# Encoder trunk on one core: low-part matmuls last, second weights loaded earlier, operand splits on VectorE

## The chip, the cores and the metric

One core of a Trainium2 chip runs the whole program in one launch. The metric is the device time of the program in microseconds (us). It is compared between the kernel before and the changed kernel.

## The reference

One layer over 2304 tokens of width 1024 (a sample of 2048 and a prompt of 256), all in float32:

```python
h = rmsnorm(x, norm1_g); p = h @ w_in              # split into q, k, v, g, lr, u, vs, xp
a_out = gla_mixer(...)                             # bidirectional gated linear attention, 512 channels
b_out = spatial_gating(gelu(u), gelu(vs), ...)     # 128x128 position mixing, 256 channels
c_out = pool_mixer(xp, ...)                        # pooling windows 2/4/8/16, 256 channels
x = x + concat([a_out, b_out, c_out]) @ w_o
h = rmsnorm(x, norm2_g)
a, up = split(h @ w_ffn_in, 2)                     # 2816 columns each
a = depthwise_conv3(a, conv_w) + conv_b
x = x + (silu(a) * up) @ w_ffn_out
y = rmsnorm(x, norm_f)
```

## The kernel before, in words

**Numbers in two parts.** A float32 operand of a large product is split into a high part (a copy rounded to TensorE's fp32r format, made by ScalarE) and a low part (the operand minus its high part, made by VectorE or GpSimd): `split`, L162. A product of two split operands is three matmuls into one PSUM bank: high by high, high by low, low by high. `mm3` (L171) issues them in that order for one slice of 128 rows, so they have the lines L172, L173 and L174 in the profile. In the products of the FFN's first matrix the same three stand in L1206 to L1208.

**Stages.** Stage 1 and stage 2 compute the mixers. `out2` (L791) then multiplies by w_o; the last of its runs shares TensorE's time with `hprep` (L964), which makes the first FFN block's token operands. The FFN works on three blocks of tokens. A block has two halves q = 0 and 1 of 384 to 386 columns, and 22 column groups j of the first matrix.

**`ffn1` (L1197)** computes one j by seven products of sums (a Strassen scheme) over four slices kk, 84 matmuls in all. Weight operands are A11, S1 to S4, A12, A22, token operands B11, T1 to T4, B22, B21. `astep` makes one weight operand some products ahead: raw load on SP's queue, high part on ScalarE, low part on GpSimd for S1 to S4 and on VectorE for the rest. In block 0 GpSimd also forms the sums S1 to S4 (L1121). After product 4 VectorE adds bank pD into `u3` (L1215). Product 7 (A22 by T4) writes on in the same bank pD, so its first matmul waits until that add has read it. `gate` (L1220) then runs conv, SiLU and the product on ScalarE and VectorE, and splits the result into uh and ul (L1234, L1236).

**`ffn2` (L1299)** multiplies a part, that is 3 or 4 consecutive j's (`PARTS`), by the second matrix: 8 output groups t, each for q = 0 and q = 1. `loadw2` (L1261) loads a weight group into the two-buffered tile rg, `prepw2` (L1266) splits it into gh (ScalarE) and, two ticks later, gl (VectorE). `before` (L1275) does this for the first two groups while the last `ffn1` ahead of the part runs. There are 21 parts. In the last part of a block the first two groups go in an interleaved order (`late`).

**Block borders.** While the last `ffn1` and last `ffn2` part of a block run, `bload` (L1075) loads the next block's token operands, four pairs p by four slices kk, in the order and at the ticks of `BORDER` (L54), and splits them: high on ScalarE, low on VectorE for p = 0 and 2 and on GpSimd for p = 1 and 3 (L1097). `finish` (L1340) normalises and stores a block's halves; for the very last half `last_norm` (L1377) does so after the last matmul.

**Order of the work.** All queues run in program order. Side work sits in generators on a `Pipe` (L94); `yield d` means "go on d ticks later", and there is one tick for every three matmuls.

Of the kernel before, what the change touches and what calls it, by code (L numbers as in the profile page):

```python
# [26 lines left out]
NJ = DFF // P  # L27
# [20 lines left out]
GD0 = (2, 2, 2, 5, 2, 2)  # L48
GF0 = (0, 1, 1, 2, 1, 1)
GD1 = (2, 2, 2, 2, 2, 2)  # L50
GF1 = (1, 1, 1, 2, 1, 4)
HP = (5, 3, 3, 3)
XG = 30
BORDER = ((0, 2, 13), (1, 2, 16), (2, 2, 19), (3, 2, 22), (0, 0, 42), (0, 1, 45), (1, 0, 48), (1, 1, 52),  # L54
          (2, 0, 56), (2, 1, 60), (3, 0, 64), (3, 1, 68), (0, 3, 78), (1, 3, 82), (2, 3, 86), (3, 3, 90))
BM = (12, 9, 1, 6, 3)
MAN = ("DVE", "Activation", "Pool", "SP")
G1 = (0, 512, 896, 1312)
# [64 lines left out]
def trunk(ctx: ExitStack, tc: tile.TileContext, xT, wa, wb, gw2, gb, rows, wsT, plw, wo, w1, w2, vec, cst, yT):  # L123
# [85 lines left out]
    if True:  # L209
# [8 lines left out]
        xs, post = {}, {}  # L218
# [298 lines left out]
    if True:  # L517
# [273 lines left out]
        def out2(u, get, between=None, begun=None):  # L791
            mh, ml = get()
            n = len(tiles_of[u]) * P
            width = 256
            alloc = lambda name: box2["acc"].tile([P, 256], F32, tag=name, name=name, bufs=AB[name])
            acc = [] if between else [alloc("acc") for _ in range(0, n, width)]

            def sums(c, xf):
                for a, o in zip(acc, range(0, n, width)):
                    w = min(width, n - o)  # L800
                    sq = alloc("sq") if c else a
                    SC.activation(sq[:, 0:w], xf[:, o:o + w], AF.Square)
                    yield 1
                    if c:
                        V.tensor_tensor(out=a[:, 0:w], in0=a[:, 0:w], in1=sq[:, 0:w], op=ALU.add)

            for c in range(KD):
                oh, ol, xr = wx.pop("h"), wx.pop("l"), wx.pop(c)
                pw_ = pmt("pw") if c or not begun else begun
                for k in range(KD):  # L810
                    if c or not begun or k < 4:
                        mm3(pw_[:, 0:n], oh[:, k], ol[:, k], mh[:, k, 0:n], ml[:, k, 0:n], k == 0 and (c > 0 or not begun),
                            k == (3 if begun and not c else KD - 1))
                    if c + 1 < KD and k in (0, 1):
                        wo_split(c + 1, k)
                    if c + 1 + look(u) < KD and k in (3, 5):
                        wo_load(u, c + 1 + look(u), k // 2 - 1)
                    if c + 1 < KD and k == 6:
                        wx[c + 1] = xr_load(u, c + 1)
                    opipe.tick()  # L820
                    (pipe if between else hpipe).tick()
                xf = xr.rearrange("p a t -> p (a t)")[:, 0:n]
                V.tensor_tensor(out=xf, in0=pw_[:, 0:n], in1=xf, op=ALU.add)
                if c + 1 < KD:
                    opipe.add(store(d_x[u][:, c], xf), 1)
# [75 lines left out]
    if True:  # L901
# [173 lines left out]
        def bload(bi, box):  # L1075
            w = box["w"] = width_of(BLOCKS[bi])
            B = box["B"] = btiles()
            got = {}

            def load(kk, p):  # L1080
                m = 2 if p < 3 else 1
                got[kk, p] = xtmp("b")[:, 0:m, 0:w]
                SY.dma_start(out=got[kk, p], in_=d_b[bi, kk][:, 2 * p:2 * p + m, 0:w])

            todo = [(kk, p) for kk, p, _ in BORDER]
            for kk, p in todo[:NX - 1]:
                load(kk, p)
            at = 0
            for n, (kk, p, tick) in enumerate(BORDER):
                if tick > at:  # L1090
                    yield tick - at
                    at = tick
                m = 2 if p < 3 else 1
                hi, src = B[p][:, 0, 0:m, kk, 0:w], got.pop((kk, p))
                SC.activation(hi, src, AF.Copy)
                yield 1
                (GP if p % 2 else V).tensor_tensor(out=B[p][:, 1, 0:m, kk, 0:w], in0=src, in1=hi.bitcast(F32), op=ALU.subtract)  # L1097
                yield 1
# [98 lines left out]
        def ffn1(i, j, box, us):  # L1197
# [2 lines left out]
            fast = j == NJ - 1  # L1200

            def prod(bank, a, b, start):
                for kk in range(4):
                    st = start and kk == 0
                    o, ah, al, bh, bl = bank[:, 0:w], A[a][:, 0, kk], A[a][:, 1, kk], B[BP[b][0]][:, 0, BP[b][1], kk, 0:w], B[BP[b][0]][:, 1, BP[b][1], kk, 0:w]
                    TE.matmul(o, ah, bh, start=st, stop=False, skip_group_check=True)  # L1206
                    TE.matmul(o, ah, bl, start=False, stop=False, skip_group_check=True)  # L1207
                    TE.matmul(o, al, bh, start=False, stop=kk == 3, skip_group_check=True)  # L1208
                    if kk == 0:
                        astep()  # L1210
                    pipe.tick()
                    hpipe.tick()

            def add(out, a, b):
                V.tensor_tensor(out=out, in0=a, in1=b, op=ALU.add)  # L1215
# [56 lines left out]
            yield 2  # L1272
            V.tensor_tensor(out=gl[:, 0:n], in0=rv, in1=gh[:, 0:n].bitcast(F32), op=ALU.subtract)  # L1273

        def before(jobs):  # L1275
            yield 1
            loadw2(jobs[0])
            loadw2(jobs[1])
            yield 12
            begin(prepw2(jobs[0]))  # L1280
            yield 5
            begin(prepw2(jobs[1]))
            yield 2
            loadw2(jobs[2])
            loadw2(jobs[3])

# [12 lines left out]
        def ffn2(jobs, todo, xs, us, no, accs=None, scaled=False, late=False):  # L1299
# [1 line left out]
            n = jobs[0][1]  # L1301
            g = {t: gw.pop(jobs[t]) for t, _ in todo}
            py = {(t, q): (ps if q else pmt)("py") for t, sel in todo for q in sel}
            order = [(t, q, k) for t, sel in todo for q in sel for k in range(n)]
            if late:
                a, b = range(n - 1), range(n)
                order = [(t, q, k) for t, q, ks in ((0, 1, a), (0, 0, a), (0, 1, b[-1:]), (1, 1, b), (0, 0, b[-1:]), (1, 0, b))
                         for k in ks]
            for at, (t, q, k) in enumerate(order):
                x2, c, j0 = xs[q], jobs[t][2], jobs[t][0]  # L1310
                uh, ul = us[j0 + k][q]
                gh, gl = g[t]
                mm3(py[t, q][:, 0:no], gh[:, k], gl[:, k], uh[:, 0:no], ul[:, 0:no], k == 0, k == n - 1)
                if late:
                    if (t, q, k) == (0, 0, n - 1):
                        begin(prepw2(jobs[2]))
                    if at == len(order) - 1:
                        loadw2(jobs[4])
                elif t and at == 0 and t + 1 < len(jobs):
                    begin(prepw2(jobs[t + 1]))  # L1320
                elif t and at == min(4, len(order) - 1) and t + 3 < len(jobs):
                    loadw2(jobs[t + 3])
                pipe.tick()
                bpipe.tick()
                if k < n - 1:
# [51 lines left out]
        def last_norm(blk, q, xs, no, acc):  # L1377
# [14 lines left out]
            SC.activation(col(k), col(k), AF.Copy, scale=vc[:, V_NF + k:V_NF + k + 1])  # L1392
            V.scalar_tensor_tensor(out=r[:, 0:nb], in0=pm[:, 0:nb], scalar=1.0 / D, in1=r[:, 0:nb], op0=ALU.mult, op1=ALU.add)
            GP.tensor_tensor(out=r[:, 0:nb], in0=r[:, 0:nb], in1=mhalf[:, 0:nb], op=ALU.pow)
            for b, c0 in enumerate(starts):
                n = min(P, no - b * P)
                SC.activation(dg[:, b * P:b * P + n], ident[:, P - n:P], AF.Copy, scale=r[:, b:b + 1])
            pipe.flush()
            TE.matmul(pr, ones, dg, start=True, stop=True)
            SC.activation(sq, pr, AF.Copy)  # L1400
            for ks, eng, src, dma in (((0, 1), V, pr, SY), ((2, 3), V, pr, SY), ((6, 7), GP, sq, SC), ((4, 5), V, pr, SY)):
                for k in ks:
# [15 lines left out]
        xs = {}  # L1418
# [7 lines left out]
        for bi, blk in enumerate(BLOCKS):  # L1426
# [5 lines left out]
            for q, n in enumerate(PARTS):  # L1432
# [6 lines left out]
                while todo and todo[0] < min(j0 + n + 1, NJ):  # L1439
# [101 lines left out]
```

## Time and profile before

| | us |
|---|---|
| median of 3 runs (lowest, highest) | 2427.66 (2427.52, 2676.5) |
| profiled execution, its own time | 2424.24 |
| its span, first to last instruction | 2422.5 |
| PE busy in it | 2366.8 |

The profile is of one execution. Its own time lies 1.7 us over its span; the profiled execution is 3.4 us under the median. Engines are PE (TensorE), PEld (its weight loads), DVE (VectorE), ACT (ScalarE), POOL (GpSimd) and SP (the queue that issues most DMAs). "PE fD L1206 <- DVE u L1215" means that a matmul of line 1206 into tile fD stood still until VectorE's instruction of line 1215 had written tile u.

### The profile page before, as it was taken

How to read it: one execution, taken by the hardware profiler on the slowest of the kernel's cores; microseconds unless marked ns; L12 is line 12 of the kernel's file. 1: busy time of each engine (PE TensorE's matmuls, PEld its weight loads, DVE VectorE, ACT ScalarE, POOL GpSimd, SP SyncE). 2: the span in 40 equal slices, each digit the busy share in tenths (PEclk: the TensorE clock that was granted, in tenths of full speed). 3: DMA queues.
4: the chain of work that ended last, by engine and by line, in shares of the span. 5: the costliest groups of instructions: out<-in, count | busy, mean ns of one | idle time of the engine just before them, and what ended most of it. 6: DMA issues, size and time to landing. Idle time of an engine off the chain costs nothing.

```text
span 2422.5 us, 36683 instructions
## 1 busy us (share of the span) xinstructions
PE 2366.8 (98%) x13280; PEld 2258.5 (93%) x13280; DVE 1648.8 (68%) x2899; ACT 1032.7 (43%) x1897; POOL 792.1 (33%) x745
## 2 busy tenths in 40 slices
PE   8999998999999999999999999999999999999997
PEld 7899997988988899999999999999999999999997
DVE  6776667676666786777777686666557765666555
ACT  6454444333333443433344544433336533344434
POOL 3332221111011855455454622323225512222221
PEclk9999999999999999999999999999999999999998
DMA  6343224565663754454535463444335543333323
GB/s 202 132 150 112 82 79 124 181 188 152 209 195 118 231 180 137 151 164 149 155 120 188 131 228 120 144 146 138 111 97 185 180 129 100 96 114 103 111 75 105
DMA packets 225466, 345.99 MB, mean 143 GB/s; under 512 B 25378, under 2 KB 117794, under 8 KB 225284
## 3 DMA queue, kind: packets, MB, share of 16 engines
q1 hardware_dynamic: 218260, 320.69, 42.5%
q0 software_dynamic: 6752, 22.55, 2.5%
q8 instruction: 105, 1.72, 0.3%
q14 instruction: 77, 0.63, 0.1%
q10 hardware_dynamic: 272, 0.39, 0.0%
HBM read 264.30 MB, written 79.25 MB: 142 GB/s over the span
## 4 chain that ended last, share of the span: by engine, by line
PE 81%; DVE 7%; issue 3%; DMA 3%; POOL 3%; ACT 2%; SPq 0%; DVEq 0%; POOLq 0%; ACTq 0%
PE py L174 7%; PE py L173 7%; PE py L172 7%; PE pm L172 4%; PE pm L174 3%; PE pm L173 3%; PE fA L1208 3%; PE fA L1206 3%; PE fA L1207 3%; PE fD L1206 3%; PE fD L1207 3%; PE fD L1208 3%; PE qm L172 2%; PE qm L174 2%; PE qm L173 2%
## 5 line engine op out<-in xcount | busy, mean ns | idle before, releaser
L165 POOL TENSOR_TENSOR S<-S,S 128x512 fp32r<-128x512 f32 x242 | 325.9, 1347 | 709.4 <-ACT S L164 629.5
L174 PE MATMUL py<-uh,gl 128*128 128x384 f32 (+1 forms) x1056 | 358.0, 339 | 6.0 <-DVE gl L1273 6.0
L173 PE MATMUL py<-ul,gh 128*128 128x384 f32 (+1 forms) x1056 | 357.5, 339 | 4.1 <-DVE ul L1236 4.1
L172 PE MATMUL py<-uh,gh 128*128 128x384 f32 (+1 forms) x1056 | 358.3, 339 | 0.6 <-ACT gh L1271 0.6
L1327 DVE TENSOR_TENSOR x<-py,x 128x384 f32<-128x384 f32 (+1 forms) x336 | 186.9, 557 | 180.1 <-PE py L174 178.6
L165 DVE TENSOR_TENSOR A<-A,A 128x512 fp32r<-128x512 f32 x198 | 169.1, 854 | 168.5 <-ACT A L164 147.6
L164 ACT ACTIVATE A<-A 128x512 fp32r<-128x512 f32 x198 | 124.9, 631 | 215.3 <-issue 82.9
L164 ACT ACTIVATE S<-S 128x512 fp32r<-128x512 f32 x242 | 151.9, 628 | 133.3 <-PE fE L1208 67.0
L174 PEld LDWEIGHTS py<-uh,gl 128*128 128x128 f32 x1056 | 199.2, 189 | 8.7 <-DVE gl L1273 8.7
L173 PEld LDWEIGHTS py<-ul,gh 128*128 128x128 f32 x1056 | 199.1, 189 | 5.0 <-DVE ul L1236 4.6
L172 PEld LDWEIGHTS py<-uh,gh 128*128 128x128 f32 x1056 | 199.4, 189 | 1.6 <-ACT gh L1271 0.9
L1271 ACT ACTIVATE gh<-rg 128x384 fp32r<-128x384 f32 (+1 forms) x174 | 93.6, 538 | 231.6 <-PE py L173 207.5
L1206 PE MATMUL fA<-B,A 128*128 128x386 f32 (+1 forms) x528 | 179.4, 340 | 0.0
L1208 PE MATMUL fA<-B,A 128*128 128x386 f32 (+1 forms) x528 | 179.1, 339 | 0.0
L1207 PE MATMUL fA<-B,A 128*128 128x386 f32 (+1 forms) x528 | 178.4, 338 | 0.0
L172 PE MATMUL pm<-wk,xh 128*128 128x512 f32 (+2 forms) x432 | 166.6, 386 | 6.9 <-ACT wk L167 6.6
L173 PE MATMUL pm<-wk,xh 128*128 128x512 f32 (+2 forms) x432 | 157.2, 364 | 0.1
L174 PE MATMUL pm<-wk,xl 128*128 128x512 f32 (+2 forms) x432 | 156.5, 362 | 0.4 <-DVE xl L165 0.4
L1273 DVE TENSOR_TENSOR gl<-rg,gh 128x384 fp32r<-128x384 f32 (+1 forms) x174 | 115.4, 663 | 11.5 <-ACT gh L1271 11.5
L174 PE MATMUL pw<-mh,ol 128*128 128x512 f32 (+1 forms) x320 | 117.9, 368 | 1.5 <-DVE ol L165 1.5
L172 PE MATMUL qm<-vk,xh 128*128 128x512 f32 x288 | 117.9, 409 | 0.0
L172 PE MATMUL pw<-mh,oh 128*128 128x512 f32 (+1 forms) x320 | 117.8, 368 | 0.0
(282 smaller groups left out, 6190.0 us busy)
## 6 DMA issues: line engine op xcount, KB each, us to landing
A<-in_w SPq DMA_DIRECT2D x242, 256.0 KB, 3.8
S<-ds_S SPq DMA_DIRECT2D x176, 256.0 KB, 2.7
rg<-in_w SPq DMA_DIRECT2D x144, 192.0 KB, 2.5
xt<-in_xT SPq DMA_DIRECT2D x35, 512.0 KB, 4.2
ds_S<-S SPq DMA_DIRECT2D x66, 256.0 KB, 2.1
rawo<-dw SPq DMA_DIRECT2D x64, 256.0 KB, 4.4
rg<-in_w SPq DMA_DIRECT2D x30, 256.0 KB, 2.9
dx<-xr SPq DMA_DIRECT2D x24, 256.0 KB, 2.5
```

The source lines that it names most:

```text
L164: SC.activation(hi, src, AF.Copy)
L165: (eng or V).tensor_tensor(out=lo, in0=src, in1=hi.bitcast(F32), op=ALU.subtract)
L172: TE.matmul(out, lh, rhs_h, start=first, stop=False)
L173: TE.matmul(out, lh, rhs_l, start=False, stop=False)
L174: TE.matmul(out, ll, rhs_h, start=False, stop=last)
L1206: TE.matmul(o, ah, bh, start=st, stop=False, skip_group_check=True)
L1207: TE.matmul(o, ah, bl, start=False, stop=False, skip_group_check=True)
L1208: TE.matmul(o, al, bh, start=False, stop=kk == 3, skip_group_check=True)
L1271: SC.activation(gh[:, 0:n], rv, AF.Copy)
L1273: V.tensor_tensor(out=gl[:, 0:n], in0=rv, in1=gh[:, 0:n].bitcast(F32), op=ALU.subtract)
L1327: V.tensor_tensor(out=x2[:, c, 1:1 + no], in0=py[t, q][:, 0:no], in1=x2[:, c, 1:1 + no], op=ALU.add)
```

## The change

Six edits:

1. `out2`: the low-by-high matmul of slice k is issued two slices later.
2. `prod` in `ffn1`: the twelve matmuls of a product go as four high by high, four high by low, four low by high. Ticks and `astep` stay at the same count of matmuls.
3. `ffn2`: for each t all matmuls with gh come first for both halves, then those with gl. The `late` order is rewritten in that sense, with uses of the last j's ul as late as the order allows.
4. `first2` and `before`: the first two loads of rg move from tick 1 of the last `ffn1` ahead of a part to tick 8 of the one before it. Their splits move from ticks 13 and 18 to ticks 3 and 8 (gl two ticks later in each case), the next two loads from tick 20 to tick 12. `GF1` makes the last j's ul three ticks sooner.
5. `bload`: all low parts on VectorE; `BORDER` spreads the 16 splits over ticks 13 to 104 in another order.
6. `last_norm`: `pipe.flush()` comes before the diagonal factors, these are made alternately by ScalarE and VectorE, and each 128-column piece has its own matmul.

```diff
-GF1 = (1, 1, 1, 2, 1, 4)
+GF1 = (1, 1, 1, 2, 1, 1)
-BORDER = ((0, 2, 13), (1, 2, 16), (2, 2, 19), (3, 2, 22), (0, 0, 42), (0, 1, 45), (1, 0, 48), (1, 1, 52),
-          (2, 0, 56), (2, 1, 60), (3, 0, 64), (3, 1, 68), (0, 3, 78), (1, 3, 82), (2, 3, 86), (3, 3, 90))
+BORDER = ((0, 2, 13), (1, 2, 17), (2, 2, 21), (3, 2, 38), (0, 0, 44), (1, 0, 49), (2, 0, 54), (3, 0, 59),
+          (0, 1, 66), (1, 1, 72), (2, 1, 78), (3, 1, 84), (0, 3, 92), (1, 3, 96), (2, 3, 100), (3, 3, 104))
@@ out2
-                    if c or not begun or k < 4:
-                        mm3(pw_[:, 0:n], oh[:, k], ol[:, k], mh[:, k, 0:n], ml[:, k, 0:n], ...)
+                    kn = 4 if begun and not c else KD
+                    if k < kn:
+                        for r in (mh, ml):
+                            TE.matmul(pw_[:, 0:n], oh[:, k], r[:, k, 0:n], start=k == 0 and r is mh and kn == KD, stop=False)
+                        for e in (range(k - 2, k - 1) if k < kn - 1 else range(k - 2, k + 1)):
+                            if e >= 0:
+                                TE.matmul(pw_[:, 0:n], ol[:, e], mh[:, e, 0:n], start=False, stop=e == kn - 1)
@@ bload
-                (GP if p % 2 else V).tensor_tensor(out=B[p][:, 1, 0:m, kk, 0:w], in0=src, in1=hi.bitcast(F32), op=ALU.subtract)
+                V.tensor_tensor(out=B[p][:, 1, 0:m, kk, 0:w], in0=src, in1=hi.bitcast(F32), op=ALU.subtract)
@@ ffn1, prod
+                for n in range(12):
+                    kk, (ia, ib) = n % 4, ((0, 0), (0, 1), (1, 0))[n // 4]
+                    TE.matmul(o, A2[:, ia, kk], B[p][:, ib, e, kk, 0:w], start=start and n == 0, stop=n == 11,
+                              skip_group_check=True)
+                    if n == 2:
+                        astep()
+                    if n % 3 == 2:
+                        pipe.tick()
+                        hpipe.tick()
@@ before
-        def before(jobs):
-            yield 1
+        def first2(jobs):
+            yield 8
             loadw2(jobs[0])
             loadw2(jobs[1])
-            yield 12
+
+        def before(jobs):
+            yield 3
             begin(prepw2(jobs[0]))
             yield 5
             begin(prepw2(jobs[1]))
-            yield 2
+            yield 4
             loadw2(jobs[2])
             loadw2(jobs[3])
@@ ffn2
+            H, M, L = 0, 1, 2
+            if late:
+                a, z = range(n - 1), n - 1
+                runs = [((0, 1), a, (H, M)), ((0, 0), a, (H, M)), ((0, 1), a, (L,)), ((0, 0), a, (L,)), ((1, 1), a, (H, M)),
+                        ((1, 1), a, (L,)), ((0, 1), (z,), (H, L)), ((1, 1), (z,), (H, L)), ((0, 1), (z,), (M,)),
+                        ((1, 1), (z,), (M,)), ((0, 0), (z,), (H, L, M)), ((1, 0), range(n), (H, M)), ((1, 0), range(n), (L,))]
+            else:
+                runs = [((t, q), range(n), f) for t, sel in todo for f in ((H, M), (L,)) for q in sel]
...
+                TE.matmul(py[at][:, 0:no], gv[f == L][:, k], u[f == M][:, 0:no], start=left[at] == 3 * n, stop=left[at] == 1)
...
@@ last_norm
+            pipe.flush()
             for b, c0 in enumerate(starts):
                 n = min(P, no - b * P)
-                SC.activation(dg[:, b * P:b * P + n], ident[:, P - n:P], AF.Copy, scale=r[:, b:b + 1])
-            pipe.flush()
-            TE.matmul(pr, ones, dg, start=True, stop=True)
+                d, e = dg[:, b * P:b * P + n], ident[:, P - n:P]
+                if b % 2:
+                    V.tensor_scalar(out=d, in0=e, scalar1=r[:, b:b + 1], scalar2=None, op0=ALU.mult)
+                else:
+                    SC.activation(d, e, AF.Copy, scale=r[:, b:b + 1])
+                TE.matmul(pr[:, b * P:b * P + n], ones, d, start=True, stop=True, skip_group_check=True)
@@ main loop, ahead of each ffn1
+                    if j == min(j0 + n, NJ - 1) - 1:
+                        pipe.add(first2(jobs))
```

## Rows read from the trace of the kernel before

**Rows 1.** The page: busy us of each engine, share of the span, instructions.

```profile
PE 2366.8 (98%) x13280; PEld 2258.5 (93%) x13280; DVE 1648.8 (68%) x2899; ACT 1032.7 (43%) x1897; POOL 792.1 (33%) x745
```

**Rows 2.** Windows A:B in us: length, busy us of PE, PEld, DVE, ACT, POOL, PEclk, DMA share, GB/s.

```profile
786.00:896.00 110.00, 104.28 (x519) 93.98 (x519) 90.53 (x103) 52.45 (x100) 83.32 (x63) 0.99 0.70 219
2060.00:2160.00 100.00, 100.00 (x567) 100.00 (x566) 63.29 (x107) 43.52 (x80) 26.79 (x20) 1.00 0.36 114
```

**Rows 3.** PE's waits, whole span: total us, times, longest.

```profile
PE fD L1206 <- DVE u L1215: 7.8, 5, 2.0
...
PE py L174 <- DVE gl L1273: 6.0, 8, 2.2
PE py L173 <- DVE ul L1236: 4.1, 2, 2.1
...
PE pr L1399 <- ACT acc L1397: 2.8, 1, 2.8
```

**Rows 4.** PE's waits from 786 to 1300 us (end of out2, most of block 0).

```profile
PE py L174 <- DVE gl L1273: 4.8, 5, 2.2
PE fD L1206 <- DVE u L1215: 4.0, 3, 1.9
PE pw L174 <- DVE ol L165: 1.5, 2, 0.8
PE fE L1208 <- POOL S L165: 0.7, 1, 0.7
PE py L172 <- ACT gh L1271: 0.6, 1, 0.6
```

**Rows 5.** Window just after the stall at 1327 us; columns as in Rows 2.

```profile
1330.50:1333.50 3.00, 3.00 (x12) 3.00 (x11) 0.44 (x1) 0.53 (x1) 0.00 (x0) 0.50 0.00 0
```

**Rows 6.** PE's timeline at 1330 us: start, duration, line, tiles.

```profile
1330.85 0.52 PE L172 MATMUL py<-uh,gh 128*128 128x384 f32 x1
1331.17 0.52 PE L173 MATMUL py<-ul,gh 128*128 128x384 f32 x1
```

**Rows 7.** Timelines of SP, ACT and DVE at 1421 us, block 1.

```profile
1415.01 1.05 SPq L1264 DMA_DIRECT2D rg<-in_w  x2
...
1421.93 0.52 ACT L1271 ACTIVATE gh<-rg 128x384 fp32r<-128x384 f32 x1 [4.86 <-DMA rg<-in_w]
...
1422.48 0.56 DVE L1273 TENSOR_TENSOR gl<-rg,gh 128x384 fp32r<-128x384 f32 x1 [2.82 <-ACT gh L1271]
1422.96 0.55 DVE L1215 TENSOR_TENSOR u<-fD,e 128x386 f32<-128x386 f32 x1
```

**Rows 8.** DVE's timeline at 1035 us, block 0.

```profile
1030.96 1.31 DVE L165 TENSOR_TENSOR A<-A,A 128x512 fp32r<-128x512 f32 x1 [0.86 <-issue]
...
1035.87 1.65 DVE L1273 TENSOR_TENSOR gl<-rg,gh 128x384 fp32r<-128x384 f32 x1
1037.43 0.55 DVE L1215 TENSOR_TENSOR u<-fD,e 128x386 f32<-128x386 f32 x1
...
1039.59 0.54 DVE L1273 TENSOR_TENSOR gl<-rg,gh 128x384 fp32r<-128x384 f32 x1
```

**Rows 9.** Groups of PE by line and shape: count, busy us, mean ns.

```profile
L1208 PE MATMUL fA<-B,A 128*128 128x386 f32 x352 | 119.4, 339 | 0.0
...
L1207 PE MATMUL fA<-B,A 128*128 128x386 f32 x352 | 118.7, 337 | 0.0
```

**Rows 10.** Line 1097, border splits: duration ns min/median/max, first and last start.

```profile
L1097 DVE TENSOR_TENSOR B<-b,B x16: 954/1100/2634, 1317.5 to 1870.3; 128x772 fp32r<-128x772 f32 x8, 128x776 fp32r<-128x776 f32 x8
...
L1097 POOL TENSOR_TENSOR B<-b,B x16: 1013/1450/2642, 1338.0 to 1885.5; 128x772 fp32r<-128x772 f32 x4, 128x386 fp32r<-128x386 f32 x4, 128x776 fp32r<-128x776 f32 x4, 128x388 fp32r<-128x388 f32 x4
```

**Rows 11.** Timeline of the tail, ACT and PE.

```profile
2409.77 1.17 ACT L1397 ACTIVATE acc<-ident,rt 128x128 f32<-128x128 f32 x4 [2.08 <-POOL rt L1394]
...
2411.00 1.66 PE L1399 MATMUL pr<-acc,ones 128*128 128x386 f32 x2 [2.85 <-ACT acc L1397]
```

**Rows 12.** Chain of waits at the end of out2: start, us, what.

```profile
811.65 2.82 POOL B L165 x3
```

More of the change, by code (lines that the diff above doesn't have):

```diff
@@ L810, in out2 @@
                 for k in range(KD):
-                    if c or not begun or k < 4:
-                        mm3(pw_[:, 0:n], oh[:, k], ol[:, k], mh[:, k, 0:n], ml[:, k, 0:n], k == 0 and (c > 0 or not begun),
-                            k == (3 if begun and not c else KD - 1))
+                    kn = 4 if begun and not c else KD
[5 more added lines that the diff above has]
+                                TE.matmul(pw_[:, 0:n], ol[:, e], mh[:, e, 0:n], start=False, stop=e == kn - 1)
                     if c + 1 < KD and k in (0, 1):
@@ L1202, in prod @@
             def prod(bank, a, b, start):
[L1203 to L1209, printed above, removed]
+                o, A2, (p, e) = bank[:, 0:w], A[a], BP[b]
+                for n in range(12):
[3 more added lines that the diff above has]
+                    if n == 2:
                         astep()
-                    pipe.tick()
-                    hpipe.tick()
+                    if n % 3 == 2:
+                        pipe.tick()
+                        hpipe.tick()
             def add(out, a, b):
@@ L1303, in ffn2 @@
             py = {(t, q): (ps if q else pmt)("py") for t, sel in todo for q in sel}
-            order = [(t, q, k) for t, sel in todo for q in sel for k in range(n)]
+            H, M, L = 0, 1, 2
             if late:
[L1306 to L1313, printed above, removed]
+                a, z = range(n - 1), n - 1
[4 more added lines that the diff above has]
+                runs = [((t, q), range(n), f) for t, sel in todo for f in ((H, M), (L,)) for q in sel]
@@ L1314, in ffn2 @@
+            order = [(at, k, f) for at, ks, fs in runs for k in ks for f in fs]
+            left = {at: 3 * n for at in py}
+            for no_, (at, k, f) in enumerate(order):
+                (t, q), x2 = at, xs[at[1]]
+                c, j0 = jobs[t][2], jobs[t][0]
+                u, gv = us[j0 + k][q], g[t]
+                TE.matmul(py[at][:, 0:no], gv[f == L][:, k], u[f == M][:, 0:no], start=left[at] == 3 * n, stop=left[at] == 1)
+                left[at] -= 1
                 if late:
-                    if (t, q, k) == (0, 0, n - 1):
+                    if at == (0, 0) and not left[at]:
@@ L1316, in ffn2 @@
                         begin(prepw2(jobs[2]))
-                    if at == len(order) - 1:
+                    if no_ == len(order) - 1:
                         loadw2(jobs[4])
-                elif t and at == 0 and t + 1 < len(jobs):
+                elif t and no_ == 2 and t + 1 < len(jobs):
                     begin(prepw2(jobs[t + 1]))
-                elif t and at == min(4, len(order) - 1) and t + 3 < len(jobs):
+                elif t and no_ == min(14, len(order) - 1) and t + 3 < len(jobs):
@@ L1322, in ffn2 @@
                     loadw2(jobs[t + 3])
-                pipe.tick()
-                bpipe.tick()
-                if k < n - 1:
+                if no_ % 3 == 2:
+                    pipe.tick()
+                    bpipe.tick()
+                if left[at]:
                     continue
-                V.tensor_tensor(out=x2[:, c, 1:1 + no], in0=py[t, q][:, 0:no], in1=x2[:, c, 1:1 + no], op=ALU.add)
+                V.tensor_tensor(out=x2[:, c, 1:1 + no], in0=py[at][:, 0:no], in1=x2[:, c, 1:1 + no], op=ALU.add)
```

## The prediction

> **What bounds the kernel now.** I read the page first, then the windows by stretch, then PE's waits, then the timelines around the longest waits. The page shows PE busy 2366.8 of 2422.5 us [rows 1]; the next engine, VectorE, has 68%. So PE's own stream sets the time, and an edit of order can win only what PE stands still, 55.7 us in all. The steady stretch of a later block shows PE busy 100.00 of 100.00 us with 567 matmuls, 0.176 us each [rows 2]: there is nothing to win inside a block. What is left sits at places. From 786 to 896 us, the end of `out2` and the first `ffn1`s of block 0, PE is busy 104.3 of 110 us while VectorE has 90.5 and GpSimd 83.3 [rows 2]. The list of waits names the rest: product 7 for `u3` 7.8 us, `ffn2` for gl 6.0 and for ul 4.1, the last broadcast for its diagonal factors 2.8 [rows 3]. Of these, 4.8 of gl and 4.0 of `u3` lie before 1300 us, with 1.5 for `out2`'s low parts, 0.7 for an S operand's low part and 0.6 for gh [rows 4]. A stall can cost twice: after the one at 1327 us the granted clock is 0.50, the lower level of 1.2 GHz, for at least 3 us [rows 5], and matmuls then start 0.32 us apart [rows 6].
>
> All terms go against the profiled execution's own 2424.24 us, which stands 3.4 us under the median of 2427.66; the forecast is the median less the same sum.
>
> **The parts, one by one.**
>
> *gl later (edit 3).* In a group of three j's the first matmul with gl was the 3rd and becomes the 13th; with four j's it becomes the 17th. Ten matmuls at 0.176 are 1.8 us of new slack. The eight waits are at most 2.2 us long [rows 3], so only the longest leaves some 0.4: **-5.6 us**; ends -6.0 and, if VectorE simply stays late, -1.2 (those outside block 0, 6.0 less 4.8 [rows 3, 4]).
>
> *gh.* The buffer of gh is now free six matmuls (1.1 us) before the group ends, so the 0.6 us wait [rows 4] goes: **-0.6**; ends -0.6 and 0.
>
> *ul (edits 3 and 4).* In the `late` order the last j's ul was first used by the 20th matmul and now by the 32nd: 12 x 0.176 = 2.1 us. `GF1` issues it three ticks, nine matmuls, 1.6 us sooner. Together 3.7 us against waits of at most 2.1: **-4.1**. The half clock at 1330 us goes too: 3.0 us at 0.32 are 9.4 matmuls, each 0.144 too slow: **-1.4**. Ends: -5.5 and 0. What is next is the last j's uh, used by the 19th matmul before and by the 28th now.
>
> *Loads of rg sooner (edit 4).* At 1421 us the chain is plain: rg issued at 1415.0, ScalarE waits 4.86 us for it, VectorE stands behind with gl for 2.82, and `u3`, queued behind gl, comes late to product 7 [rows 7]. An `ffn1` has 28 ticks, so tick 8 of the one before is 21 ticks or 11 us sooner than tick 1: the 4.86 are covered, and the two waits outside block 0, 7.8 less 4.0, go [rows 3, 4]: **-3.8**; ends -3.8 and 0. Each part moves four DMA issues on SP's queue, in all 84: the first two past the operand loads of 21 ticks, the others past those of 8. A pair takes 1.05 us to issue [rows 7]; the operand loads behind them are made several products ahead, which hides that; with that cover gone it would be 1.05 us in such a part. The third and fourth load wait for the first two gl, now two ticks after the second gl is issued instead of none, so SP stands less.
>
> *The same move in block 0.* There VectorE is behind without help from a DMA: the gl ahead of `u3` takes 1.65 us and the second gl, after `u3`, 0.54 [rows 8]. The change puts both ahead of `u3`, but earlier, where VectorE has 0.86 us of idle time [rows 8]. `u3` then moves by between -0.9 (the idle time is used and the second gl adds nothing) and +1.65 (it adds a slow one). I take **0** for the 4.0 us of waits, nearest the sum 0.54 - 0.86; ends -5.4 (with a half clock of 1.4 after the longest) and the price of the slower rival below. Here a page bears on it. The Trainium skill, "SBUF — State Buffer", section "Who interferes with whom", says that a VectorE instruction with two SBUF inputs and a GpSimd one that reads SBUF block each other. The trace agrees: the same gl took 1.65 and 0.54 us [rows 8].
>
> *Low parts last in `out2` and `ffn1` (edits 1 and 2).* The waits they reach are 1.5 and 0.7 us [rows 4]. But in that stretch the chain of waits runs over GpSimd's splits [rows 12], and PE relieved at one place comes sooner to `u3`, which VectorE gives no sooner. I take **0**; ends -2.2 and 0. The order itself: of the three matmuls the second shares its weights with the first, and in the new order of a product no neighbours do. Lines 1207 and 1208 differ by 2 ns, 337 and 339 [rows 9], and every matmul has its own weight load, 13280 and 13280 [rows 1]. So 0, with ends of plus and minus 1848 x 2 ns = 3.7 us. The Trainium skill, "TensorE: Matmul & The Clock Gate", section "Part 2: What happens when you issue a matmul", says that weights loaded once can serve many matmuls, which speaks for the old order. By that rule the sum would be 3.7 us worse; by the rows it is not.
>
> *Border splits (edit 5).* GpSimd loses 16 instructions of 1.45 us median, VectorE gains 16 at 1.10 median, 2.63 at most [rows 10]; the eight narrow ones should be less. That is some 9 us of VectorE per border, over 40 ticks (21 us) and more. Outside block 0 VectorE is 63% busy [rows 2], which hides it: **0**. The last four, for T4, now fall in the next block's first `ffn1` at ticks 0 to 12, ahead of product 7 at tick 24, six us later. If the cover is gone, each border waits for one split: +2.6 twice, +5.3. End below: 0, no wait for B stands in the list.
>
> *Tail (edit 6).* The factors take 1.17 us for four, the broadcast 1.66 [rows 11]. The first piece can start after one factor, 0.9 us sooner, and four pieces cost some of it back: **-0.6**; ends -0.9 and +0.8 (half a broadcast for the extra starts).
>
> **Sum:** -5.6 - 0.6 - 4.1 - 1.4 - 3.8 - 0.6 = -16.1 us. The profiled execution would take 2408.1; the median **2411.6 us**.
>
> **Rivals.**
>
> *Block 0 gives its gain back.* VectorE's backlog there comes from GpSimd, not from the order, so the waits for gl and gh return one group later. For it: the slow gl in rows 8. Against: `ffn2` gives VectorE time to catch up. 5.0 us less gain: 2416.6. Chance 0.20.
>
> *Block 0 is cured as well.* The idle 0.86 us is used, `u3` comes in time, and `out2` and S waits pay: another 5.4 + 2.2 = 7.6 us: 2404.0. For it: 0.86 over 0.54. Against: GpSimd's chain [rows 12]. Chance 0.15.
>
> *Slower: the second gl ahead of `u3`.* Place: product 7 of the last `ffn1` ahead of each of block 0's six parts with three j's. Price: 1.65 us for a slow gl [rows 8] plus 1.4 of half clock, 3.05 x 6 = 18.3, and the gains of block 0 are gone: -16.1 + 5.0 + 18.3 = +7.2, 2434.9. It decides once `u3` falls behind by more than the slack that the four parts without a wait have, which no row gives. For it: both splits really go ahead of `u3`. Against: they also go earlier. Chance 0.08.
>
> *The products run slower in the new order.* +3.7: 2415.3. Chance 0.07, since the 2 ns are of the size by which equal groups differ.
>
> *The order does nothing* is not a case of its own: the waits named in rows 3 and 7 follow from it.
>
> **Numbers.** The forecast has 0.50. The range goes from the cured case, rounded down, 2403, to the first rival with the border's 5.3 and some 1 us for the tail, 2423. A difference of 2%, about 49 us, is what a measurement of this kernel can tell from no change. The waits that the edits can reach sum to 7.8 + 6.0 + 4.1 + 2.8 + 1.5 + 0.7 = 22.9 us [rows 3, 4], gh's 0.6 and two half clocks on top, so over 2% faster has 0.02; over 2% slower needs several new waits per part, 0.03; within 2% 0.95.
>
> **What would show it.** Gone from PE's waits: ul, gl outside block 0, and `u3` outside block 0; the clock stays at 1.00 at the end of block 0's last part. gl in block 0 falls under 1 us. If `u3` grows before 1300 us, the slower rival is at work; if waits for gl there stay near 4.8, the first one. The mean of the product matmuls tells the order's price: 341 ns instead of 339 would bear it out. A wait of a product for a B tile's low part after a border would show that VectorE can't hide the splits. The prediction is wrong at its root if PE's busy time per matmul moves, since all terms are waits.

## The result, and the profile after

The changed kernel takes **2408.97 us** (median of 4 runs, 2404.49 to 2411.89) beside 2427.59 for the kernel before on the same chip: a ratio of **0.993 [0.9915, 0.9945]**, 18.6 us less by the medians. One of the four executions of the kernel before took 2676.5 us, a tenth more than the others, and the ratio leaves it out. The difference counts as no change at a bound of 2%, and is faster by the interval. The forecast was 2411.6.

The profiled execution took 2410.87 us. Its page, as in [rows 1]:

```profile
span 2409.1 us, 36723 instructions
PE 2366.8 (98%) x13286; PEld 2263.4 (94%) x13286; DVE 1667.0 (69%) x2917; ACT 1030.9 (43%) x1895; POOL 772.1 (32%) x729
```

The span fell from 2422.5 us. PE does the same matmuls but for six in the tail; what changed is where it stands. That its busy time is the same to the tenth, 2366.8 us, is chance: among the kernels below it lies between 2357.9 (e13_block0_dve) and 2368.2 us (e4_tail). The list of PE's waits over the whole span (total us, times, longest), beside [rows 3]:

```profile
PE fD L1210 <- DVE u L1219: 5.2, 3, 2.2
...
PE pr L1416 <- ACT acc L1415: 2.1, 1, 2.1
...
PE pw L817 <- DVE ol L165: 0.8, 1, 0.8
...
PE py L1324 <- ACT gh L1275: 0.8, 1, 0.8
...
PE py L1324 <- ACT uh L1238: 0.6, 1, 0.6
...
PE py L1324 <- DVE gl L1277: 0.4, 1, 0.4
```

ul is gone, gl fell from 6.0 to 0.4, and `u3` stands at 5.2 us, all three waits in block 0; after 1300 us only uh and the final norm are waited for. Windows of the changed kernel (length, busy us of PE, PEld, DVE, ACT, POOL, PEclk, DMA share, GB/s):

```profile
786.00:896.00 110.00, 105.44 (x526) 95.16 (x524) 90.69 (x112) 52.14 (x101) 80.99 (x62) 0.98 0.69 218
1330.50:1333.50 3.00, 3.00 (x18) 3.00 (x18) 3.00 (x5) 2.30 (x6) 0.98 (x1) 1.00 0.02 5
2060.00:2160.00 100.00, 100.00 (x567) 100.00 (x566) 64.37 (x110) 40.75 (x75) 22.57 (x17) 1.00 0.32 100
72.50:75.50 3.00, 3.00 (x15) 3.00 (x16) 1.31 (x3) 0.77 (x2) 1.34 (x3) 0.50 0.57 214
864.50:867.50 3.00, 3.00 (x11) 3.00 (x10) 2.19 (x4) 1.23 (x2) 2.33 (x2) 0.50 0.78 197
898.50:901.50 3.00, 3.00 (x11) 3.00 (x10) 2.19 (x3) 1.23 (x2) 1.21 (x1) 0.50 0.25 94
840.00:1300.00 460.00, 453.42 (x2550) 450.74 (x2549) 344.90 (x485) 182.73 (x343) 248.43 (x176) 0.99 0.48 152
```

The first three answer to [rows 2] and [rows 5]: the later block is as full as before, and at 1330 us the granted clock is 1.00 where it was 0.50. New are half clocks, that is stretches with a granted clock of 0.50, at 72, 393 and 417 us, in code that the change doesn't touch, and at 864 and 898 us, behind two of the waits for `u3`. In block 0 the kernel before had the one at 894 us and, at the block's end, the one of [rows 5]. The last window in the kernel before:

```profile
840.00:1300.00 460.00, 449.84 (x2529) 445.30 (x2528) 340.88 (x481) 183.01 (x340) 239.22 (x173) 1.00 0.48 149
```

So profiles are best compared by the length of a block, from its first product to the next block's, as PE's timeline shows it (us). The kernel before, run beside each group on its chip, took 2427.18 (e1 to e4), 2429.72 (e5 to e8), 2427.39 (e9, e11) and 2427.26 us (e12, e13).

| Kernel | Median time | Block 0 starts | Block 0 | Block 1 |
|---|---|---|---|---|
| before | 2427.6 | 830.66 | 531.00 | 521.98 |
| after | 2408.97 | 833.80 | 524.23 | 515.41 |
| e1_order | 2418.54 | 832.94 | 524.98 | 517.71 |
| e2_loads | 2415.84 | 834.55 | 524.76 | 517.65 |
| e3_border | 2425.48 | 829.92 | 532.32 | 520.53 |
| e4_tail | 2426.98 | 832.09 | 528.68 | 523.11 |
| e5_old_product | 2407.97 | 830.44 | 523.00 | 515.48 |
| e6_gl1_after_u3 | 2407.89 | 833.28 | 525.10 | 515.42 |
| e7_old_split_ticks | 2413.77 | 834.65 | 526.91 | 515.20 |
| e8_no_sums | 2397.27 (one run) | 833.00 | 511.70 | 515.19 |
| e9_sums_dve | 2401.94 | 830.84 | 516.40 | 515.57 |
| e11_u3_first | 2414.79 | 833.30 | 527.56 | 515.19 |
| e12_before_sums | 2418.28 | 831.16 | 524.96 | 521.80 |
| e13_block0_dve | **2397.14** | 831.34 | 513.17 | 515.19 |

After against before: block 0 starts 3.1 us later (the stages ahead of `out2` end 4.0 later with their three half clocks), block 0 takes 6.8 less, block 1 6.6, block 2 2.6, the tail 0.6: -13.4 in the span. The medians differ by 5.2 more, because before's profile lay 3.4 below its median and after's 1.9 above.

The splits in block 1, ScalarE's and VectorE's timelines beside [rows 7]:

```profile
1410.92 0.51 ACT L1275 ACTIVATE gh<-rg 128x384 fp32r<-128x384 f32 x1
...
1411.46 0.56 DVE L1277 TENSOR_TENSOR gl<-rg,gh 128x384 fp32r<-128x384 f32 x1
1414.64 0.55 DVE L1277 TENSOR_TENSOR gl<-rg,gh 128x384 fp32r<-128x384 f32 x1
1416.77 0.55 DVE L1219 TENSOR_TENSOR u<-fD,e 128x386 f32<-128x386 f32 x1
```

ScalarE waits for no DMA, both gl are done ahead of `u3`, and PE doesn't wait for `u3`. The same place in block 0, VectorE beside [rows 8]:

```profile
888.24 1.57 DVE L1277 TENSOR_TENSOR gl<-rg,gh 128x384 fp32r<-128x384 f32 x1
890.67 1.32 DVE L165 TENSOR_TENSOR A<-A,A 128x512 fp32r<-128x512 f32 x1 [0.39 <-issue]
...
893.47 1.66 DVE L1277 TENSOR_TENSOR gl<-rg,gh 128x384 fp32r<-128x384 f32 x1
896.73 0.55 DVE L1219 TENSOR_TENSOR u<-fD,e 128x386 f32<-128x386 f32 x1
```

Both gl are slow and both stand ahead of `u3`, and PE waits 2.17 us for it: the place of the slower rival. But of PE's three waits for `u3` in block 0 only this one and the one at 1181 us (0.96 us) lie in the last `ffn1` ahead of a part. The other, 2.10 us at 863 us, lies in the block's second `ffn1`, before any gl is made. There a split of an A operand stands ahead of `u3`:

```profile
861.32 1.61 DVE L165 TENSOR_TENSOR A<-A,A 128x512 fp32r<-128x512 f32 x1
862.86 0.55 DVE L1219 TENSOR_TENSOR u<-fD,e 128x386 f32<-128x386 f32 x1
```

### The profile page after: what moved, and what is told of

Its sections match the earlier page's. It is cut to its first block, busy times and chain, and to the rows that moved or that the text cites. A ratio compares the mean times of both kernels' runs of the same rounds, so it can differ in the third digit from the quotient of the medians.

```text
span 2409.1 us, 36723 instructions
## 1 busy us (share of the span) xinstructions
PE 2366.8 (98%) x13286; PEld 2263.4 (94%) x13286; DVE 1667.0 (69%) x2917; ACT 1030.9 (43%) x1895; POOL 772.1 (32%) x729
## 4 chain that ended last, share of the span: by engine, by line
PE 84%; DVE 5%; DMA 3%; POOL 3%; issue 2%; ACT 2%; SPq 0%; DVEq 0%; POOLq 0%; ACTq 0%
PE py L1324 21%; PE fA L1210 10%; PE fD L1210 10%; PE fC L1210 5%; PE fB L1210 5%; PE fE L1210 5%; PE pw L814 4%; PE pm L172 3%; PE pm L173 3%; PE pm L174 3%; PE qm L172 2%; PE qm L174 2%; PE qm L173 2%; PE pw L817 2%; DMA A<-in_w 1%
## 5 line engine op out<-in xcount | busy, mean ns | idle before, releaser
L1210 PE MATMUL fA<-B,A 128*128 128x386 f32 (+1 forms) x1584 | 302.7, 340 | 0.0
L1210 PEld LDWEIGHTS fA<-B,A 128*128 128x128 f32 x1584 | 281.4, 189 | 0.6
L1340 DVE TENSOR_TENSOR x<-py,x 128x384 f32<-128x384 f32 (+1 forms) x336 | 180.1, 557 | 144.9 <-PE py L1324 143.6
L1324 PE MATMUL py<-uh,gl 128*128 128x384 f32 (+1 forms) x1056 | 216.1, 338 | 0.4 <-DVE gl L1277 0.4
L1324 PEld LDWEIGHTS py<-uh,gl 128*128 128x128 f32 x1056 | 187.8, 188 | 1.0 <-DVE gl L1277 0.7
L1210 PE MATMUL fD<-B,A 128*128 128x386 f32 (+1 forms) x792 | 153.0, 342 | 5.3 <-DVE u L1219 5.2
L1210 PE MATMUL fC<-B,S 128*128 128x386 f32 (+1 forms) x792 | 151.2, 339 | 0.0
L1210 PE MATMUL fD<-B,S 128*128 128x386 f32 (+1 forms) x792 | 150.7, 338 | 0.0
L1210 PE MATMUL fB<-B,S 128*128 128x386 f32 (+1 forms) x792 | 150.7, 339 | 0.0
L1210 PE MATMUL fE<-B,S 128*128 128x386 f32 (+1 forms) x792 | 150.7, 339 | 0.0
```

The source lines that it names most:

```text
L1210: TE.matmul(o, A2[:, ia, kk], B[p][:, ib, e, kk, 0:w], start=start and n == 0, stop=n == 11, skip_group_check=True)
L1324: TE.matmul(py[at][:, 0:no], gv[f == L][:, k], u[f == M][:, 0:no], start=left[at] == 3 * n, stop=left[at] == 1)
L1340: V.tensor_tensor(out=x2[:, c, 1:1 + no], in0=py[at][:, 0:no], in1=x2[:, c, 1:1 + no], op=ALU.add)
```

## The experiments

**The parts by themselves.** Each of the first four is the kernel before with one part of the change.

*e1_order*: the orders of `out2`, product and `ffn2` alone.

```
- mm3(...)                          # out2, prod, ffn2
+ runs = [((t, q), range(n), f) for t, sel in todo for f in ((H, M), (L,)) for q in sel]
...
```

> The kernel before with the three new matmul orders alone (out2, product, ffn2). Theory of waits by place: gl in ffn2 has 1.8 us more room, so its 6.0 us fall to about 0.4, gh's 0.6 go, the last j's ul gets 2.1 us of room against waits of 2.1 us, so at most 0.3 of its 4.1 us stay and the half clock at 1330 us goes (1.4); u3's 7.8 us stay, since VectorE's queue is unchanged. Sum 5.6 + 0.6 + 4.1 + 1.4 = 11.7 us: about 2416. Rival, VectorE simply late in block 0: its gl waits (4.8 us) move one group on, gain 6.9: about 2421. Rival, the gain is in loads and border: within 2 us of 2427.6.

2418.54 us, ratio 0.9967 [0.9953, 0.9981]. PE's waits from 786 to 1300 us, against [rows 4]:

```profile
PE fD L1210 <- DVE u L1219: 8.8, 5, 2.4
PE fE L1210 <- ACT S L164: 1.0, 1, 1.0
...
PE py L1322 <- DVE gl L1277: 0.5, 1, 0.5
```

gl falls from 4.8 to 0.5 and `u3` grows from 4.0 to 8.8: in block 0 the order alone moves the wait to another tile. The time lies between the theory's 2416 and the first rival's 2421; the wait came back at `u3`, which the theory left unchanged, and not at gl. The gain is ul, the gl waits of the later blocks, and both half clocks of block 0 (one comes at 1938 us instead).

*e2_loads*: the loads and splits of the second weights sooner, alone.

```
-GF1 = (1, 1, 1, 2, 1, 4)
+GF1 = (1, 1, 1, 2, 1, 1)
+        def first2(jobs):
+            yield 8                # in the ffn1 before
...
```

> The kernel before with the loads and splits of the second weights sooner and the last j's ul three ticks sooner, old matmul orders. Theory of waits by place: the two u3 waits of blocks 1 and 2 go (3.8 us), ul loses 1.6 of each 2.1 us wait (3.2) and with it the half clock (1.4); gl of later groups stays in the main, as their splits are started where they were: gain 8.4 us, about 2419. Rival, the loads alone set the whole gain, gl included: 15 us or more, 2412. Rival, both gl splits ahead of u3 cost as much in block 0 as is won elsewhere: 2425 to 2430, and u3's wait before 1300 us above 6 us.

2415.84 us, 0.9953 [0.9936, 0.997]. PE's waits from 1300 to 2406 us:

```profile
PE py L174 <- DVE gl L1273: 1.4, 3, 0.6
PE py L173 <- DVE ul L1236: 0.9, 1, 0.9
```

No `u3` is left there, and block 1 is 4.3 us shorter. It gained 3 us more than expected: in block 0 `u3` fell from 4.0 to 0.9, and the half clock at 894 us did not come. So with the old order the earlier splits help `u3` there, too.

*e3_border*: the border's ticks and all its splits on VectorE.

```
-(GP if p % 2 else V).tensor_tensor(out=B[p][:, 1, 0:m, kk, 0:w], ...)
+V.tensor_tensor(out=B[p][:, 1, 0:m, kk, 0:w], ...)
```

> The kernel before with the border splits all on VectorE and spread, nothing else. Theory of waits by place: no PE wait hangs on them but ul's, since VectorE has two B splits fewer between ticks 13 and 25 ahead of the last gate; ul's wait falls by about one split, 0.95 us each, and perhaps the half clock: gain 0 to 3.4 us, 2424 to 2428. Rival, the port: GpSimd's 16 splits hold VectorE up, and their removal is worth more than 4 us.

2425.48 us, 0.9993 [0.9982, 1.0003]: no difference. No wait for a B tile appears.

*e4_tail*: the last factors piecewise.

```
-TE.matmul(pr, ones, dg, start=True, stop=True)
+TE.matmul(pr[:, b * P:b * P + n], ones, d, start=True, stop=True, ...)   # in the loop over pieces
```

> The kernel before with the last factors and the last broadcast made piecewise, nothing else. Theory: the wait of 2.8 us before the broadcast falls by 0.7 to 0.9, the broadcast of 1.66 grows by some 0.2: gain 0.6 us, 2427.0. Rival: more matmul starts eat it all, 0.

2426.98 us beside 2427.18, 0.9999 [0.9984, 1.0014]: the 0.6 us can't be seen in times. They stand in after's tail (ScalarE, VectorE and PE), against [rows 11]:

```profile
2396.94 0.69 ACT L1415 ACTIVATE acc<-ident,rt 128x128 f32<-128x128 f32 x2 [2.08 <-POOL rt L1407]
2397.02 0.42 DVE L1413 TENSOR_SCALAR acc<-ident,rt 128x128 f32<-128x128 f32 x2
2397.39 1.86 PE L1416 MATMUL pr<-acc,ones 128*128 128x128 f32 x8 [2.08 <-ACT acc L1415]
```

The factors take 0.69 instead of 1.17 us, the wait falls by 0.77, and the eight pieces cost 0.20 more than the two matmuls.

**What sets `u3` in block 0.** The next four are the changed kernel with one edit each.

*e5_old_product*: the product's old order (hi·hi, hi·lo, lo·hi for each kk).

```
-for n in range(12):
-    kk, (ia, ib) = n % 4, ((0, 0), (0, 1), (1, 0))[n // 4]
+for kk in range(4):
...
```

> The changed kernel with the old order inside a product (high, low, low-by-high for each slice). Theory: inside a product the order is worth nothing but the waits for an S operand's low part (1.5 us with the old order, 0 with the new); u3 in block 0 stands by VectorE's queue, so PE that no longer waits there waits at u3: 2409 within 2 us. Rival: the new product order brings PE sooner to u3 and so costs the two half clocks of block 0: u3 before 1300 us falls from 5.2 to about 1, 2404 to 2406. Rival: the order pays in every product by its cadence: 2413 or more.

2407.97 us, 0.9914 [0.9899, 0.9929]: its interval overlaps that of the change. The order of the product is worth nothing that can be measured in times. In block 0 `u3` is waited for five times, 4.0 us in all and 1.2 at most, S costs 1.2 again, and no half clock comes; the block is 1.2 us shorter than with the change. The Trainium skill, "TensorE: Matmul & The Clock Gate", section "Part 2: What happens when you issue a matmul", says that weights loaded once can serve many matmuls. In both orders every matmul here has its own weight load (13286 of 13286), and these runs show no price of either order.

*e6_gl1_after_u3*: the second split at tick 16, behind `u3`. The next two loads follow it in the same generator, so they move too, from tick 12 to tick 20.

```
-            yield 5
+            yield 13
             begin(prepw2(jobs[1]))
```

> The changed kernel with the second group's split begun at tick 16 instead of 8 of the last ffn1 ahead of a part, so that its gl stands behind u3 on VectorE. Theory: in block 0 that gl (0.55 to 1.65 us) delays u3: u3 before 1300 us falls from 5.2 to about 2 and one half clock goes, 2404 to 2406; gl and ul stay cured, as gl of the second group is used 31 matmuls into the part. Rival: VectorE is behind for another reason, u3 stays near 5: 2409. Rival: gl of the second group is now late: waits for gl above 1.5 us, 2411.

2407.89 us, 0.991 [0.9893, 0.9926]. Inconclusive: `u3` fell to 3.6 and one half clock went, but there are four waits for gh that no theory named, 4.4 us (786 to 1300 us):

```profile
PE py L1324 <- ACT gh L1275: 4.4, 4, 2.0
PE fD L1210 <- DVE u L1219: 3.6, 3, 1.8
```

The first of them, at 904 us, shows time given back. ScalarE started that gh at 903.70 us, behind a step of `gate` that had waited for VectorE; in the changed kernel it started it at 904.88. But PE, held up less at `u3`, came for it at 903.3 instead of 907.4 us.

*e7_old_split_ticks*: loads as in the change, splits at the old ticks.

```
-            yield 3
+            yield 13
             begin(prepw2(jobs[0]))
...
```

> The changed kernel with the first two loads sooner, but their splits at the old ticks 13 and 18 and the next two loads at tick 20. Theory: blocks 1 and 2 were cured by the load being there, not by the split's tick: u3 after 1300 us stays 0; in block 0 it is as with the changed kernel or worse, 5 to 8: 2409 to 2412. Rival: the splits' ticks cured blocks 1 and 2: u3 after 1300 us is back at 3.8, 2413.

2413.77 us, 0.9934 [0.9919, 0.9949]. PE's waits from 786 to 1300 us:

```profile
PE fD L1210 <- DVE u L1219: 7.8, 5, 2.3
PE fD L1210 <- ACT S L164: 0.9, 1, 0.9
```

After 1300 us one wait of 1.0 is left for `u3`, and block 1 is as short as with the change. So in the later blocks it is mostly the early load that cures. In block 0 PE waits 7.8 us for `u3` instead of 5.2, as the theory had it (5 to 8), and the block is 2.7 us longer. By its ratio the run can't be told from the change (0.9934 and 0.993), so that the early splits help in block 0 is read from the profile alone.

*e8_no_sums*: GpSimd's 88 sums for S operands in block 0 are left out (a copy on ScalarE stands for those that don't add in place), so the output differs.

```
-            GP.tensor_tensor(out=out, in0=a, in1=b, op=o)
+            if out is not a and out is not b:
+                SC.activation(out, a, AF.Copy)
```

> The changed kernel with GpSimd's sums S1 to S4 in block 0 left out (S1 and S2 are plain ScalarE copies, S3 and S4 are unchanged tiles, so the output differs). Theory: GpSimd's two-input work holds VectorE up in block 0; without 88 sums of 1.3 to 1.7 us VectorE's 1.6 us instructions there fall to 0.55 to 0.7, u3 before 1300 us falls under 0.5 and gl and gh with it, no half clock in block 0: about 2400. Rival: VectorE's own work is too much there: u3 stays above 3, 2407 or more.

2397.27 us in one run. Window 840 to 1300 us, columns as above:

```profile
840.00:1300.00 460.00, 460.00 (x2615) 459.46 (x2614) 298.56 (x499) 211.92 (x396) 124.38 (x96) 1.00 0.51 159
```

The group of VectorE's splits of A operands in that window (count, busy us, mean ns, idle before):

```profile
L165 DVE TENSOR_TENSOR A<-A,A 128x512 fp32r<-128x512 f32 x62 | 44.2, 714 | 53.7 <-ACT A L164 53.7
```

In the changed kernel the second row was:

```profile
L165 DVE TENSOR_TENSOR A<-A,A 128x512 fp32r<-128x512 f32 x61 | 69.4, 1137 | 43.4 <-ACT A L164 36.0 <-issue 7.4
```

PE is full, no wait for `u3`, gl, gh or S is left in block 0, and VectorE's own split runs in 714 instead of 1137 ns. This points at GpSimd's sums as what made VectorE late; with work left out and one run it takes the next runs to show it.

**Can that be had without leaving work out?**

*e9_sums_dve*: the sums on VectorE (the changed kernel).

```
-            GP.tensor_tensor(out=out, in0=a, in1=b, op=o)
+            V.tensor_tensor(out=out, in0=a, in1=b, op=o)
```

> The changed kernel with block 0's sums S1 to S4 made by VectorE instead of GpSimd. Leaving the sums out took 46 us off VectorE's busy time from 840 to 1300 us; making the 80 there itself at 0.69 each costs it 55. Theory, GpSimd costs VectorE the time its two-input instructions run beside VectorE's: the two about cancel, and VectorE's queue now also waits for the raw loads of the sums: u3 before 1300 us 5 or more, 2409 to 2415. Rival, it is the length of single blocked instructions, not the sum, that makes u3 late: u3 before 1300 us under 2, 2401 to 2404.

2401.94 us, 0.9902 [0.9876, 0.9927], which still touches the interval of the change. My theory, that slower and faster VectorE work would cancel, fell; the rival's time held (2401 to 2404), with `u3` at 2.3 us, a little above the 2 that it named. Window 840 to 1300 us, and VectorE's splits of A operands in it:

```profile
840.00:1300.00 460.00, 456.41 (x2588) 454.47 (x2588) 339.14 (x574) 189.87 (x349) 125.22 (x96) 1.00 0.49 154
L165 DVE TENSOR_TENSOR A<-A,A 128x512 fp32r<-128x512 f32 x61 | 44.2, 725 | 35.7 <-ACT A L164 35.7
```

VectorE does 89 instructions more than in the changed kernel, the sums among them, and is busy 339.1 us instead of 344.9. Another rival, that the sums come sooner and so ScalarE's high parts do too, doesn't explain the splits: VectorE stands idle for ScalarE before them as long as before (35.7 and 36.0 us), and what changed is their length.

*e11_u3_first*: the changed kernel, the operand step of product 7 behind the addition of `u3`.

```
-            prod(pD, "S3", "T3", True)
+            prod(pD, "S3", "T3", True, False)
             u3 = tmp("u3")[:, 0:w]
             add(u3, pD, e1)
+            astep()
```

> The changed kernel with the weight operand that is made during product 4 begun after u3's add instead of before it, in all blocks, so that its low part (0.7 to 1.8 us on VectorE) stands behind u3. Its use is product 7, eight ticks later, and its low part is used only by the last four matmuls there. Theory, u3 in block 0 is late by what stands just ahead of it on VectorE: u3 before 1300 us falls from 5.2 to under 1 and both half clocks of block 0 go: gain 4 to 7 us, 2402 to 2405. Rival, VectorE is behind as a whole and the time is given back at the next user: waits for ul, gl or A operands' low parts of 4 us or more before 1300 us, 2409.

2414.79 us, 0.9948 [0.9928, 0.9969]: the theory fell, though both half clocks of block 0 went as it said. PE's waits from 786 to 1300 us:

```profile
PE fD L1210 <- DVE u L1219: 4.5, 3, 2.4
PE py L1325 <- ACT gh L1276: 3.1, 3, 1.7
PE fE L1210 <- ACT S L164: 1.2, 3, 0.6
```

Little comes off `u3`, and more appears at gh and S, which neither theory nor rival named: this new order of VectorE's queue did not help.

*e12_before_sums*: the kernel before with e9's edit alone.

```
-            GP.tensor_tensor(out=out, in0=a, in1=b, op=o)
+            V.tensor_tensor(out=out, in0=a, in1=b, op=o)
```

> The kernel before with block 0's sums S1 to S4 on VectorE, none of the six edits. Theory, from the run with the sums moved in the changed kernel: single VectorE instructions blocked behind GpSimd's are what makes PE wait in block 0, whatever the order; of the 10.1 us there (gl 4.8, u3 4.0, S 0.7, gh 0.6) with a half clock of 1.4 some 6 to 9 go, u3 under 1 and gl under 3: 2419 to 2421. Rival, the edits have to be there first: u3 and gl before 1300 us stay above 7 together, 2425 or more.

2418.28 us, 0.9966 [0.9952, 0.9979]. Block 0 is 6.0 us shorter and block 1 as before: one line is worth about half of the change. Before 1300 us `u3` falls from 4.0 to 0.2 and gl from 4.8 to 1.8, while the low parts of S, still GpSimd's, grow from 0.7 to 2.6. PE's waits from 1300 us on are those of before:

```profile
PE py L173 <- DVE ul L1236: 4.1, 2, 2.1
PE fD L1206 <- DVE u L1215: 3.9, 2, 2.1
```

*e13_block0_dve*: the changed kernel with e9's edit, and block 0's S splits on VectorE too.

```
-            split(t[:, 0], t[:, 1], src, eng=GP if n[0] == "S" else V)
+            split(t[:, 0], t[:, 1], src, eng=GP if n[0] == "S" and i >= NJ else V)
```

> The changed kernel with block 0's sums and the low parts of its S operands all on VectorE, so that GpSimd does next to nothing in block 0. Theory: the rest of the waits before 1300 us (u3 2.3, gh 1.1, S 0.3 with the sums alone moved) is GpSimd's too and goes: 2398 to 2400. Rival: VectorE, busy 339 of 460 us with the sums, gets some 55 us more less what the contention gave back, and is late by its own work: u3 or gl of 4 us or more before 1300 us, 2404 to 2410.

**2397.14 us** (2395.15 to 2399.69), 0.9882 [0.986, 0.9905]: better than both kernels, its interval clear of the change's. Of the waits for `u3`, gl, gh and S from 786 to 1300 us one is left:

```profile
PE fD L1210 <- DVE u L1219: 1.1, 1, 1.1
```

Window 840 to 1300 us:

```profile
840.00:1300.00 460.00, 458.85 (x2606) 457.89 (x2605) 371.23 (x663) 194.63 (x353) 13.71 (x12) 1.00 0.51 158
```

VectorE's splits of A operands there:

```profile
L165 DVE TENSOR_TENSOR A<-A,A 128x512 fp32r<-128x512 f32 x62 | 42.6, 687 | 10.7 <-ACT A L164 10.4
```

VectorE is busier (371 of 460 us) and, but for one wait, in time; GpSimd is nearly idle.

## Why the prediction was right, and where it was not

The frame held: PE's work is constant and only its standing changed. The parts:

- **gl: -5.6 forecast, 6.0 to 0.4 measured.** Right in size. The reason holds outside block 0. In block 0 e1_order shows that the order alone hands the wait to `u3`; the loads and splits sooner take most of that off again (e2_loads).
- **gh: -0.6 forecast, 0.6 to 0.8 measured.** Wrong in its mechanism: in both kernels ScalarE didn't wait for the buffer there. gh stood in its queue behind ten small instructions of 2.59 us, with no idle time before it. ScalarE's timeline, two rows of the kernel before and two of the changed one:

```profile
969.85 2.59 ACT L1040 ACTIVATE rb<-ident,r 128x1 f32<-128x1 f32 x10
...
973.16 0.51 ACT L1271 ACTIVATE gh<-rg 128x384 fp32r<-128x384 f32 x1
...
974.01 2.59 ACT L1044 ACTIVATE rb<-ident,r 128x1 f32<-128x1 f32 x10
...
977.34 0.51 ACT L1275 ACTIVATE gh<-rg 128x384 fp32r<-128x384 f32 x1
```

- **ul: -4.1 and -1.4 forecast.** The wait went and the clock stays at 1.00, but uh, named as next, took 0.6: -3.5.
- **Loads: -3.8 outside block 0.** Right: gone in e2_loads, down to 1.0 in e7_old_split_ticks with loads alone.
- **`u3` in block 0: 0 forecast, 4.0 to 5.2 measured**, with two half clocks behind these waits where there was one. The prediction weighed the splits alone, between idle time that is used and a slow gl that is added. By themselves they win (4.0 to 0.9 in e2_loads), though in the changed kernel slow gl stand ahead of `u3` at 893 us. What the term left out is the order: PE, no longer held up before, comes sooner to `u3` (8.8 in e1_order). What I had as a backlog has a cause that e8_no_sums and e9_sums_dve show: with GpSimd's sums the same split takes VectorE 1137 ns, without them 714, with the sums on VectorE 725. The Trainium skill, "SBUF — State Buffer", section "Who interferes with whom", says that a VectorE instruction with two SBUF inputs and a GpSimd one that reads SBUF block each other; the runs agree, by those numbers. The prediction used it for one gl and not for the whole block, where 12 us more lay (2408.97 to e13's 2397.14).
- **`out2`, S and the product's order: 0 forecast.** ol fell from 1.5 to 0.8 and S's 0.7 went, 1.4 of the 2.2 that the lower end held. Product matmuls take the same mean time, as the group of the changed kernel shows against [rows 9]:

```profile
L1210 PE MATMUL fA<-B,A 128*128 128x386 f32 x1056 | 201.6, 339 | 0.0
```

- **Border: 0.** Right by e3_border: 16 more splits on VectorE with no wait behind any. The group after, beside [rows 10]:

```profile
L1101 DVE TENSOR_TENSOR B<-b,B x32: 548/956/2060, 1318.2 to 1882.1; 128x772 fp32r<-128x772 f32 x12, 128x776 fp32r<-128x776 f32 x12, 128x386 fp32r<-128x386 f32 x4, 128x388 fp32r<-128x388 f32 x4
```

- **Tail: -0.6.** -0.6 in the profile.

The sum was 2.5 us short of the medians' difference. One piece of that has a row. The stall at 1327 us in the kernel before, PE's timeline:

```profile
1327.22 0.44 PE L172 MATMUL py<-uh,gh 128*128 128x384 f32 x1
1329.73 0.44 PE L173 MATMUL py<-ul,gh 128*128 128x384 f32 x1 [2.07 <-DVE ul L1236]
```

The starts are 2.51 us apart where 0.18 is usual, so PE lost 2.33; the wait counts 2.07, from the modelled end of the matmul before. Matmuls overlap, so each wait row is 0.16 to 0.26 too small (0.34 or 0.44 less 0.18). From `ffn1` on, 17 waits for `u3`, gl, ul, uh, gh and S became 6: 11 x 0.2 is about 2 us that the sum left out. The rest is within the scatter.

That the sum came so near is in part luck. Its misses in `u3` with one more half clock (1.2 and 1.4), gh (0.8) and uh (0.6) make 4.0 us; S (0.7) and the overlap (about 2), which it left out on the other side, give most of that back.

Of the rivals, "block 0 gives its gain back" is half true: its cause, GpSimd, is the one found, and in e1_order block 0's wait does come back, but at `u3` and not at gl one group later; the loads sooner hold it off. "Block 0 is cured" did not happen here and is what e9 and e13 nearly do, for another reason: not the order, but GpSimd's share of VectorE's time. That the mechanism is contention and not the count of VectorE's instructions follows from e9 and e13, where VectorE has more to do.

**Open:** block 0's length differs by 3.6 us among kernels with nearly the same code there (before, e3, e4), and the intervals of e5, e6, e7 and e11 all overlap that of the change, so these four are weak evidence; why gh becomes late in e11 was not tried.

## What to carry to other kernels

Work handed from VectorE to GpSimd isn't free for VectorE: compare the mean of the same VectorE instruction with GpSimd busy and idle before the work is placed, and move it back where VectorE has idle time. A new order on the bounding engine removes a wait only if the engine it waits for is in time on average; if that engine is late, look for what slows it. A load must have landed before the in-order engine reaches its first user, since what queues behind that user pays too.

## What the runs showed of the hardware

- From 840 to 1300 us, which holds 82 of the 88 sums, each sum on GpSimd cost VectorE at least (344.9 - 298.6) / 82 = 0.56 us of longer instructions; e8_no_sums did 14 VectorE instructions more in that time. VectorE does one itself in 0.69 to 0.84 us (means in e9_sums_dve). In the changed kernel 34 of VectorE's 61 splits of A operands took over 1.2 us there; with the sums on VectorE 2 of 61, with the S splits there too none.
- The half clock doesn't follow every stall: it came behind those of some 2 us at 891 and 1327 us in the kernel before, and not behind others as long (at 1117, 1421 and 1851 us). Stages that no edit touched had none to three such stretches from kernel to kernel. Among the kernels with the old `out2` they end up to 4.4 us apart (their last matmul into tile qm starts at 780.1 us in e3_border, at 784.5 in e2_loads), which is as large as most parts of this change.
